# The samples' queries and scores turned in 32x32 blocks on VectorE, and another order of the pieces ahead of the feed-forward

## The chip, the cores and the metric

The kernel runs on one core of a Trainium2 chip. The metric is the device time of one execution in microseconds (us); the lower the better. A time is the median of several runs; a profile is one further execution, taken with the hardware profiler, and has a time and a span (first to last instruction) of its own.

## The reference

One layer of a decoder trunk for a prompt of 1024 tokens and 8 samples of one token each, all in float32, model width 1024:

```python
h = rmsnorm(x, g_mix); u = h @ w_in                # 512 pool, 512 value, 512 gate columns
ya = pool_mixer(...)                               # trailing means over 2/4/8/16, a map per group
yb = conv_mixer(...)                               # GLU, causal depthwise conv of 31, LayerNorm, silu
x = x + concat([ya, yb]) @ w_out
x = x + cross_attn(rmsnorm(x, g_attn), mk, mv)     # 4 heads of 256, 256 memory tokens
h = rmsnorm(x, g_ffn)
x = x + (silu(h @ w_gate) * (h @ w_up)) @ w_down   # 2816 hidden columns
y = rmsnorm(x, g_final)
```

The prompt attends to keys and values that are computed from `mem_prompt`. Each of the 8 samples attends to a cache of its own (`cache_mem_k`, `cache_mem_v`: 256 tokens, 4 heads of 256). The other outputs are the new pooling and convolution states and the prompt's keys and values.

## The kernel before

Activations lie with channels on the 128 partitions and tokens along the free axis: 1032 columns (T), 1024 of the prompt and the 8 samples last. Each matmul of two float32 operands is made of three: an operand is split into a high part (a rounded copy) and a low part (what is left), and hi x hi, hi x lo and lo x hi are added up (`PASSES`). So weights and activations are split all the time: `split` makes the high part on ScalarE or GpSimd and the low part by a subtraction on VectorE or GpSimd; `split_by_dma` makes the high part and its negative on ScalarE or GpSimd, and the low part by a DMA from GpSimd's queue that adds the original onto the negative. `BY_DMA` lists the weight blocks that take the second way. The feed-forward and its down projection use sums of blocks with fewer products (seven in place of eight).

The instructions are not issued in the order in which they stand in the code. `ORDER` is a list of pieces, each a letter and a number ("q3", "S12"); the pieces are run in that order and add tasks to a `Program` with an engine (or a choice of engines), a cost, what they read and write, and a priority by their place. `Program.order` then plans the tasks with these costs: at each step it takes the engine that can start first, and on it the earliest task, the one with the smaller place among those within a small slack; it also assigns buffers, of which each tag has a fixed number (`w` 2, `raw` 3, `scr` 3, `op` 19, `rows` 2; in PSUM `mm` 2 of three banks and `ms` 2 of one). The instructions of each engine are emitted in that order, and each engine runs its own list in order, waiting where an operand isn't there. All plain DMAs go through SP's queue, in order too. `LEAD` says how many blocks ahead of its use a weight block is prepared.

The pieces around the change:

- `q` (`q_group`): queries, 72 matmuls each; the 8 sample columns of each are copied to `qs` (L1004). `S` (`scores`, L1023), `T` (`p_transpose`, L1062) and `P` (`pv`, L1081) are the prompt's scores, the turning of the probabilities and the products with the values; the results are split into `oo` (L1085, L1086).
- `a` (`s_query`, L1090): for head h, two transposes on TensorE (L1095) turn `qs` (128 channels x 8 samples, two halves) into rows of 8 samples x 256 in PSUM; VectorE copies them out (L1099), and a DMA writes them to DRAM (`qd`).
- `b` (`s_scores`) and `d` (`s_values`), both by `s_dots`: a DMA reads the rows back, broadcast to all partitions; two DMAs bring pieces of the cache; VectorE multiplies and sums up (L1120), one sample at a time. Most heads do this in two halves of four samples with the three `scr` buffers; three of the eight (head, cache) pairs use `op` buffers and all eight samples (`ALL_SAMPLES`).
- `c` (`s_softmax`): the scores `ssc` (128 tokens x 8 samples, two halves) are turned by two transposes on TensorE (L1133); maximum (L1141), exponential (L1145) and normalising (L1150) follow on the 8 rows, which a DMA writes to DRAM (`pd`) for the values.
- `e` (`s_out`): the samples' results, in `qs` again (`os_`), are split into the last 8 columns of `oo`.
- `B` (`out_b`): second part of the mixer's output projection; makes x1, splits it for the queries, and adds its squares up. `f` (`token_factors`): the RMS factors of the tokens. `o` (`proj_o`): attention output projection, blocks 0 to 7 of 72 matmuls; for blocks 0 and 4, the first two thirds of the columns come first, and the third third, which holds the samples, after. It adds the residual (L1192) and the squares (x2sq) for the factors `Rf` (piece `r`, L510).
- `x`, `y`, `z` make the operands of the feed-forward, `h` its first weights, `i` and `j` its first products (L1323). At the end, L1665 is the last part of the down projection, with the weight blocks w_dn 16 to 19 and w_dn2 0 and 1.

Of the kernel before, what the change touches and what calls it, by code (L numbers as in the profile page):

```python
# [8 lines left out]
F32 = mybir.dt.float32  # L9
F32R = mybir.dt.float32r  # L10
AF = mybir.ActivationFunctionType
ALU = mybir.AluOpType
# [248 lines left out]
def hybrid_step_kernel(ctx: ExitStack, tc: tile.TileContext, io):  # L261
# [78 lines left out]
    pd = dram.tile([HEADS, NS, NMEM], F32, name="pd")  # L340

# [6 lines left out]
    nc.gpsimd.memset(cnt, 1.0)  # L348
# [41 lines left out]
    def split_by_dma(dst, key, src, n, r, again, again_keys, pool_too=False):  # L390
# [11 lines left out]
        add({"Pool": 0.6}, lambda e: e.dma_start(dst(1), again(), accum_op=ALU.add), [key(1)] + again_keys, [key(1)], nbytes=4 * P * n)  # L402

# [553 lines left out]
    def out_b(n):  # L957
# [11 lines left out]
        square_into(lambda: xss1[:], (xss1,), lambda: x1[j][:, i], [xk], T, n == 0, f"x1sq{n}")  # L969
# [24 lines left out]

    qop = [op_r(f"qo{n}") for n in range(KT)]
# [3 lines left out]
    def q_group(n):  # L999
# [4 lines left out]
        add({"DVE": 0.07}, lambda e: e.tensor_copy(qs[:, n], ps[:, 2, CW - NS : CW]), all3(ps), [("qs", n)])  # L1004
# [85 lines left out]
    def s_query(h):  # L1090
        ps = ms_buf(f"sq{h}")

        def emit(e):
            for dt in range(2):
                e.transpose(ps[:NS, dt * P : (dt + 1) * P], qs[:, 2 * h + dt], ident)  # L1095
# [3 lines left out]
        add({"DVE": 0.33}, lambda e: e.tensor_copy(rows[:], ps[:NS, :256]), [(ps,)], [(rows,)])  # L1099
        dma(lambda: qd[h], lambda: rows[:], 8192, r=[(rows,)], w=[("qd", h)])  # L1100

    def s_dots(h, scratch, skey, cache, out, okey):
# [5 lines left out]
        for first in range(0, NS, count):  # L1108
# [3 lines left out]
                P * count * 1024, r=[skey], w=[(bc,)])  # L1112
# [12 lines left out]
    def s_scores(h):  # L1125
        s_dots(h, qd, ("qd", h), "cache_k", lambda m: ssc[:, h, m], ("ssc", h))

    def s_softmax(h):
        ps = ms_buf(f"ss{h}")

        def emit(e):
            for m in range(2):
                e.transpose(ps[:NS, m * P : (m + 1) * P], ssc[:, h, m], ident)  # L1133

        add({"PE": 0.25}, emit, [("ssc", h, m, half) for m in range(2) for half in range(2)], [(ps,)])
        st = buf(f"sst{h}", "sst", (NS, 4))
        rs = r16[:NS, 16:17]
        prow = buf(f"prow{h}", "rows", (NS, 256))

        def top(e):  # L1140
            e.tensor_reduce(st[:, 0:1], ps[:NS, :256], axis=AX.X, op=ALU.max)  # L1141
            e.scalar_tensor_tensor(st[:, 1:2], st[:, 0:1], -1.0, rs, ALU.mult, ALU.mult)
# [703 lines left out]
```

## Time and profile before

| | |
|---|---|
| median of 3 runs | 1224.16 us (1222.42 to 1229.16) |
| the profiled execution | 1224.89 us |
| its span, first to last instruction | 1223.0 us |
| TensorE (PE) busy, matmuls | 1200.1 us, 7720 |
| VectorE (DVE), ScalarE (ACT), GpSimd (POOL) busy | 927.2, 527.8, 243.3 us |
| data moved by DMA | 181.80 MB, mean 149 GB/s |

In the profile's lines an instruction is named by its line in the code, its engine and its operands by the program's names, "out<-in". "x8" is a count. In a list of waits stand the total, the number and the longest; in a timeline, the start and the duration in us, and in brackets the idle time before it and what ended it. SPq and POOLq are the queues' own instructions, which issue DMAs. `ld` behind PE is the loading of weights into the array, which runs beside the matmuls.

### The profile page before, as it was taken

To read this page: it belongs to the slowest core of one execution; us is meant where nothing else is said; L and a number is where in the kernel's file an instruction comes from. 1 tells how busy PE (TensorE), PEld (TensorE's weight loads), DVE (VectorE), ACT (ScalarE), POOL (GpSimd) and SP (SyncE) were. 2 spreads that over 40 slices of the span, in tenths; PEclk is the share of its full clock that TensorE was granted. 3 is DMA by queue.
4 is the path that set the end of the run, shared out by engine and by line. 5 is a ranking of instruction groups with operands and counts; after the bars stand their busy time and mean duration, and the time that the engine had idled before them with its cause. 6 is when DMAs were issued, how large, how long until landed. Compare 5 with 4: busy or idle time off the path is not lost.

```text
span 1223.0 us, 19412 instructions
## 1 busy us (share of the span) xinstructions
PE 1200.1 (98%) x7720; PEld 1122.0 (92%) x7720; DVE 927.2 (76%) x1549; ACT 527.8 (43%) x722; POOL 243.3 (20%) x296
## 2 busy tenths in 40 slices
PE   8999999999999999999999999999999999999997
PEld 8999988999999979989999999999999999999786
DVE  7999999767258886679777777777867788888654
ACT  7765556455134533444222322233222365545433
POOL 3568841231111102111000000000000124332101
PEclk9999999999999999999999999999999999999998
DMA  7335678226395773421232233222313698668612
GB/s 287 86 72 114 143 210 250 105 104 194 115 294 182 240 280 103 156 104 61 104 113 79 96 113 113 105 78 96 122 70 111 217 317 239 172 183 220 155 50 90
DMA packets 60875, 181.80 MB, mean 149 GB/s; under 512 B 7857, under 2 KB 11633, under 8 KB 59505
## 3 DMA queue, kind: packets, MB, share of 16 engines
q1 hardware_dynamic: 53824, 157.92, 37.1%
q0 software_dynamic: 6960, 22.65, 10.5%
q8 instruction: 60, 0.98, 0.3%
q14 instruction: 31, 0.25, 0.1%
HBM read 146.76 MB, written 33.78 MB: 148 GB/s over the span
## 4 chain that ended last, share of the span: by engine, by line
PE 76%; DVE 4%; DMA 2%; issue 2%; ACT 1%; POOL 0%; DVEq 0%; POOLq 0%; ACTq 0%
PE pr L1323 48%; PE ps L480 7%; PE po L480 7%; PE fd L1665 5%; PE ob L480 4%; PE oa L480 3%; PE sc L1023 1%; PE pv L1081 1%; DMA w<-in_w_q 1%; DMA raw<-in_w_out_a 1%; DMA w<-in_w_dn 0%; DVE spcache_k L1120 0%; DMA spcache_k<-in_cache_k 0%; DVE oo L1086 0%; DVE pT L1067 0%
## 5 line engine op out<-in xcount | busy, mean ns | idle before, releaser
L1323 PEld LDWEIGHTS pr<-ab,wTb 128*128 128x128 f32 x1056 | 132.1, 188 | 3.6
L1323 PE MATMUL pr<-ab,wTa 128*128 128x260 f32 x1056 | 133.6, 282 | 0.0
L1323 PE MATMUL pr<-ab,wTb 128*128 128x260 f32 x1056 | 133.3, 282 | 0.0
L1323 PEld LDWEIGHTS pr<-ab,wTa 128*128 128x128 f32 x1056 | 130.7, 189 | 2.0 <-DVE su L1339 0.3
L1323 PE MATMUL pr<-ab,wG 128*128 128x512 f32 x528 | 128.8, 392 | 0.0
L1339 DVE TENSOR_TENSOR su<-pr,su 128x520 f32<-128x520 f32 (+1 forms) x112 | 77.5, 694 | 57.5 <-PE pr L1323 57.3
L480 PE MATMUL ps<-xop,w 128*128 128x344 f32 x720 | 114.1, 320 | 0.0
L480 PEld LDWEIGHTS ps<-xop,w 128*128 128x128 f32 x720 | 113.6, 188 | 0.0
L1323 PEld LDWEIGHTS pr<-ab,wG 128*128 128x128 f32 x528 | 96.3, 188 | 18.8
L1323 PEld LDWEIGHTS pr<-hb,dV 128*128 128x128 f32 x768 | 98.4, 188 | 5.8 <-ACT dV L373 0.9
L1323 PE MATMUL pr<-hb,dV 128*128 128x260 f32 x768 | 100.2, 283 | 1.0 <-DVE dV L384 0.5
L480 PE MATMUL ps<-xq,w 128*128 128x344 f32 x576 | 94.8, 321 | 0.3 <-DMA w<-in_w_q 0.3
L480 PEld LDWEIGHTS po<-oo,w 128*128 128x128 f32 x576 | 90.9, 188 | 0.6 <-DVE oo L1086 0.4
L480 PE MATMUL po<-oo,w 128*128 128x344 f32 x576 | 91.4, 320 | 0.0
L480 PEld LDWEIGHTS ps<-xq,w 128*128 128x128 f32 x576 | 90.7, 188 | 0.7 <-DMA w<-in_w_q 0.6
L684 DVE SCALAR_TENSOR_TENSOR cacc<-glu,vec,cacc 128x511 f32<-128x511 f32 (+14 forms) x116 | 76.9, 739 | 0.0
L1323 PE MATMUL pr<-hb,dW 128*128 128x512 f32 x288 | 74.2, 394 | 0.0
L1665 PE MATMUL fd<-ho,w 128*128 128x260 f32 (+1 forms) x432 | 69.8, 322 | 0.7 <-DMA w<-in_w_dn 0.6
L1665 PEld LDWEIGHTS fd<-ho,w 128*128 128x128 f32 x432 | 61.7, 188 | 8.4 <-DMA w<-in_w_dn 1.1
L373 ACT ACTIVATE w<-raw 128x1024 fp32r<-128x1024 f32 (+1 forms) x35 | 32.9, 944 | 77.1 <-issue 19.7
L1323 PE MATMUL pr<-ab,wU 128*128 128x512 f32 x264 | 64.8, 394 | 0.0
L1350 POOL MEMSET su<- 128x16 f32 x22 | 2.5, 111 | 310.0 <-PE pr L1323 244.3
(306 smaller groups left out, 2183.9 us busy)
## 6 DMA issues: line engine op xcount, KB each, us to landing
gr<-in_w_gu SPq DMA_DIRECT2D x44, 512.0 KB, 3.6
hb<-su SPq DMA_DIRECT2D x8, 1040.0 KB, 4.6
hs<-hb SPq DMA_DIRECT2D x16, 520.0 KB, 6.7
dr<-in_w_dn SPq DMA_DIRECT2D x16, 512.0 KB, 3.7
spcache_k<-in_cache_k SPq DMA_DIRECT2D x12, 512.0 KB, 5.2
hs<-hb SPq DMA_DIRECT2D x12, 512.0 KB, 4.7
raw<-in_w_in SPq DMA_DIRECT2D x10, 512.0 KB, 3.7
hb<-he SPq DMA_DIRECT2D x8, 520.0 KB, 3.2
```

What stands on the lines that cost most here:

```text
L373: e.activation(dst(0), src(), AF.Copy, scale=1.0 if gain is None else gain)
L480: e.matmul(ps[:, c, :CW], w[:, wi, cols], x[:, xi, c * CW : (c + 1) * CW], start=first and p == 0, stop=last and p == 2)
L684: e.scalar_tensor_tensor(acc[h][:, n:], src[:, : HALF - n], w, acc[h][:, n:], ALU.mult, ALU.add)
L1023: e.matmul(bank()[:, i * NMEM : (i + 1) * NMEM], qop[2 * h + dt][:, qi, tt * P : (tt + 1) * P], kk[:, ki, 2 * (h % 2) + dt], start=(dt == ...
L1081: e.matmul(ps[:, c], v[:, vi, m, col : col + P], pT[h][m][:, pi, sl], start=(m == 0 and p == 0), stop=(m == 1 and p == 2))
L1323: e.matmul(bank(c), w[:, wi, cols(j)], xs[0](j, xi)[:, c * n : (c + 1) * n], start=onto is None and j == 0 and p == 0, stop=j == nj - 1 an ...
L1339: from_sums(sums, "DVE", dve, lambda e, src, sl: e.tensor_tensor(as_banks(o(sl), src), src, as_banks(a(sl), src), op), [akey], [okey])
L1350: add({"Pool": 0.12}, lambda e: e.memset(o(), 0.0), [], keys)
L1665: e.matmul(view(i), w[:, wi, col : col + P], hops[k][:, xi, half, lo - half * HALF + i * width // count : lo - half * HALF + (i + 1) * wid ...
```

## The change

`qs` and `ssc` get another layout (head, sample, half), so that the 16 columns of a head lie together, and are set to zero at the start. `s_query` and `s_softmax` no longer use TensorE and PSUM: VectorE turns 128 x 32 columns (those of a head and its neighbour) in 32x32 blocks. In the result a partition holds 32 channels (or tokens) of one sample and half. For the queries, four DMAs of 2 KB (one for each group of 32 partitions) write the rows in order to `qd`; for the scores, one DMA writes the whole 128 x 32 tile to a new DRAM tensor `sd`, and a second one reads the 8 x 256 rows back in order; the softmax then works on these rows in SBUF.

The squares in `out_b` and `proj_o` become pieces of their own (`t`, `u`), and the last third of blocks 0 and 4 of `proj_o` too (`E`), so that `ORDER` can place them. `ORDER`, `BY_DMA` and `LEAD` get other entries.

```diff
 ORDER = (
-    "m5 A3 n0 g1 v1 g2 v2 m3 m7 m4 C0 g3 v3 C1 m0 s1 s0 A2 m1 D0 A0 m2 m6 A1 K0 K1 V1 W3 D1 W0 K2 s3 s2 W1 W2 C2 M0 M3 V0 "
-    "C3 D2 D3 M1 L0 M2 K3 O0 O1 O3 O2 B0 B1 B2 B3 q0 q1 Z0 a0 b0 f0 q2 c0 q3 a1 b1 c1 S4 S0 S6 S5 S2 q4 q5 a2 Y0 S7 S1 S3 "
-    "S8 T0 d0 T3 T4 S9 T1 S10 T2 d1 q6 T8 q7 S11 T11 T5 P1 S12 T10 a3 S15 S13 T9 S14 T12 b2 T7 T6 T13 b3 T14 T15 c3 c2 d2 "
-    "P4 e1 e0 P5 P2 P3 P7 d3 P0 e3 P6 e2 o0 o4 o1 y0 o5 x0 x1 x4 o2 h0 x5 z0 h1 y1 o6 o3 x2 o7 z1 h2 y2 x6 x3 y3 x7 z2 r0 "
-    "h3 i1 i0 j0 z3 j1"
+    "m1 n0 m5 A3 m7 g1 m3 v1 g2 v2 g3 v3 A1 C0 C1 A2 s1 m2 s0 D0 m6 A0 m4 m0 K1 D1 V1 K0 W3 W0 K2 s3 W1 C2 s2 M0 W2 M3 V0 "
+    "C3 D2 D3 M1 L0 K3 M2 O0 O1 O2 O3 B3 B0 t0 B1 t1 t2 B2 t3 t4 t5 q0 t6 t7 q1 Z0 f0 q3 a0 b0 q2 a1 b1 S0 S4 c0 c1 S6 Y0 "
+    "S5 S7 q5 S3 q4 a2 S2 S1 T0 S8 d0 T2 T3 T4 S9 T1 d1 b2 T5 S10 q6 T8 q7 S11 P1 T11 S12 S13 S14 T10 S15 T9 T12 T7 T6 a3 "
+    "b3 c3 T14 c2 d2 e0 e2 e1 P0 d3 T15 T13 P4 P5 P2 P6 P7 P3 o0 o4 e3 E0 E4 x4 y0 o5 x0 u0 u4 o1 u1 z0 u5 x5 y1 h0 h1 o2 "
+    "o6 u2 u6 y2 o3 x2 u3 o7 h2 h3 x1 x3 x6 z1 i1 u7 r0 y3 x7 z2 i0 j0 z3 j1"
 )
-BY_DMA = {"w_in": (3, 4, 6, 7, 9, 10, 11), "w_k": (2, 3, 5, 6), "w_o": (4, 5, 6), "w_out_a": (1,), "w_out_b": (3,), "w_q": (4, 5, 6), "w_v": (0, 7), "w_dn": (17, 18, 19), "w_dn2": (1,)}
+BY_DMA = {"w_in": (3, 4, 5, 6, 7, 9, 10, 11), "w_k": (2, 3, 5, 6), "w_o": (0, 2, 4, 6), "w_out_a": (1, 3), "w_out_b": (0,), "w_q": (2, 3, 4, 5, 6), "w_v": (0, 1, 6, 7), "w_dn": (18,), "w_dn2": (1,)}
-LEAD = {"w_k": 2, "w_v": 3, "w_out_a": 15, "w_q": 15, "w_in": 1, "w_out_b": 12, "w_o": 8}
+LEAD = {"w_k": 2, "w_v": 3, "w_out_a": 14, "w_q": 18, "w_in": 2, "w_out_b": 10, "w_o": 5}
...
-    qs = const.tile([P, KT, NS], F32, name="qs")
-    os_ = qs
-    ssc = const.tile([P, HEADS, 2, NS], F32, name="ssc")
+    qs = const.tile([P, HEADS, NS, 2], F32, name="qs")
+    ssc = const.tile([P, HEADS, NS, 2], F32, name="ssc")
...
+    sd = dram.tile([HEADS, P, 32], F32, name="sd")
...
+    nc.gpsimd.memset(qs, 0.0)
+    nc.gpsimd.memset(ssc, 0.0)
...
+    def turned(name, src, h, r):
+        t = buf(f"{name}{h}", "rows", (P, 32))
+        add({"DVE": 0.12}, lambda e: e.transpose(t[:], src[:, min(h, 2) : min(h, 2) + 2].rearrange("p h b i -> p (h b i)")), r, [(t,)])
+        return t
...
     def s_query(h):
-        ps = ms_buf(f"sq{h}")
-        def emit(e):
-            for dt in range(2):
-                e.transpose(ps[:NS, dt * P : (dt + 1) * P], qs[:, 2 * h + dt], ident)
-        add({"PE": 0.25}, emit, [("qs", 2 * h), ("qs", 2 * h + 1)], [(ps,)])
-        rows = buf(f"qrow{h}", "rows", (NS, 256))
-        add({"DVE": 0.33}, lambda e: e.tensor_copy(rows[:], ps[:NS, :256]), [(ps,)], [(rows,)])
-        dma(lambda: qd[h], lambda: rows[:], 8192, r=[(rows,)], w=[("qd", h)])
+        t = turned("qt", qs, h, [("qs", 2 * h), ("qs", 2 * h + 1)])
+        for g in range(4):
+            dma(lambda g=g: qd[h].rearrange("b (i g d) -> (b i) g d", i=2, g=4)[:, g], lambda g=g: t[32 * g + 16 * (h == 3) : 32 * g + 16 * (h == 3) + 16], 2048,
+                r=[(t,)], w=[("qd", h, g)])
...
     def s_softmax(h):
-        ps = ms_buf(f"ss{h}")
-        def emit(e):
-            for m in range(2):
-                e.transpose(ps[:NS, m * P : (m + 1) * P], ssc[:, h, m], ident)
-        add({"PE": 0.25}, emit, [("ssc", h, m, half) for m in range(2) for half in range(2)], [(ps,)])
+        t = turned("st", ssc, h, [("ssc", h, m, half) for m in range(2) for half in range(2)])
+        dma(lambda: sd[h], lambda: t[:], 128 * P, r=[(t,)], w=[("sd", h)])
...
+        dma(lambda: prow[:].rearrange("b (m g d) -> b m g d", m=2, g=4),
+            lambda: sd[h].rearrange("(g z b m) d -> z b m g d", g=4, z=2, b=NS)[int(h == 3)], 8192, r=[("sd", h)], w=[(prow,)])
...
-            e.tensor_reduce(st[:, 0:1], ps[:NS, :256], axis=AX.X, op=ALU.max)
+            e.tensor_reduce(st[:, 0:1], prow[:], axis=AX.X, op=ALU.max)
```

More of the change, by code (lines that the diff above doesn't have):

```diff
@@ L402, in split_by_dma, with took @@
         add({"Pool": 0.6}, lambda e: e.dma_start(dst(1), again(), accum_op=ALU.add), [key(1)] + again_keys, [key(1)], nbytes=4 * P * n)
+    def took(name):
+        state[name] = state.get(name, -1) + 1
+        return state[name]
     def square_into(total, tkey, src, r, n, first, name, at=None):
@@ L968, in out_b, with x1_square @@
         dma(lambda: x1d[n], lambda: x1[j][:, i], 4 * P * T, r=[xk], w=[("x1d", n)])
-        square_into(lambda: xss1[:], (xss1,), lambda: x1[j][:, i], [xk], T, n == 0, f"x1sq{n}")
+    def x1_square(n):
+        j, i = n // 2, n % 2
+        square_into(lambda: xss1[:], (xss1,), lambda: x1[j][:, i], [(x1[j], i)], T, not took("t"), f"x1sq{n}")
     def token_factors():
@@ L1155, in s_values @@
     def s_values(h):
[L1156 removed]
+        s_dots(h, pd, [("pd", h)], "cache_v", lambda dt: qs[:, h, :, dt], ("os", h))
     def s_out(h):
@@ L1186, in proj_o, with spans_of, o_out, x2_square @@
         ps = mm_buf(f"po{n}")
-        for spans in ((0, 1), (2,)) if n in (0, 4) else ((0, 1, 2),):
+        def spans_of(spans):
+            parts = [0] * (0 in spans) + [1] + ["s"] * (2 in spans)
             for k in range(KT):
-                parts = ([0] if 0 in spans else []) + ([1, "s"] if 2 in spans else []) + ([0, 1] if spans == (0, 1) else [])
                 okeys = [(oop[k], p, part) for part in parts for p in range(2)]
                 step3(ps, w, wkeys, block_cols(k), oop[k], k, k == 0, k == KT - 1, spans, okeys)
+        if n in (0, 4):
+            spans_of((0, 1))
+            late_o[n] = lambda: (spans_of((2,)), o_out(n, ps))
+        else:
+            spans_of((0, 1, 2))
+            o_out(n, ps)
+    late_o = {}
+    def o_out(n, ps):
+        j, i = n % 4, n // 4
+        xk = [(xa[j], i, h) for h in range(2)]
         add({"DVE": dve(T)}, lambda e: e.tensor_tensor(ch3(xa[j][:, i]), ps[:, :, :CW], ch3(xa[j][:, i]), ALU.add), all3(ps) + xk, xk)
         dma(lambda: x2d[n], lambda: xa[j][:, i], 4 * P * T, r=xk, w=[("x2d", n)])
-        square_into(lambda: xss2[:], (xss2,), lambda: xa[j][:, i], xk, T, n == 0, f"x2sq{n}")
+    def x2_square(n):
+        j, i = n % 4, n // 4
+        square_into(lambda: xss2[:], (xss2,), lambda: xa[j][:, i], [(xa[j], i, h) for h in range(2)], T, not took("u"), f"x2sq{n}")
     def quarter(j, i, h):
```

19 lines of the change are left out of this document (9 added, 10 removed).

## The prediction

> **What bounds the kernel now.** I read the page first (busy times and the slices), then what TensorE waited for, then the stretches in which it waited.
>
> ```profile
> span 1223.0 us, 19412 instructions
> PE 1200.1 (98%) x7720; PEld 1122.0 (92%) x7720; DVE 927.2 (76%) x1549; ACT 527.8 (43%) x722; POOL 243.3 (20%) x296
> PEclk9999999999999999999999999999999999999998
> ```
>
> TensorE is busy for 1200.1 of 1223.0 us at a full granted clock, so the time is its work plus 22.9 us of idle. The list of its waits says where 14.3 us of these are:
>
> ```profile
> PE psg L480 <- ACT w L373: 5.2, 1, 5.2
> PE pv L1081 <- DVE oo L1086: 2.1, 2, 1.2
> PE Rf_ps L510 <- DVE xss L411: 1.8, 1, 1.8
> PE kps L850 <- DMA w<-in_w_k: 1.1, 2, 0.7
> PE pmap L870 <- ACT yf L874: 0.9, 1, 0.9
> PE fd L1665 <- DMA w<-in_w_dn: 0.6, 1, 0.6
> PE fin_ps L1699 <- ACT fsq L1680: 0.6, 1, 0.6
> PE pr L1323 <- DVE dV L384: 0.5, 1, 0.5
> PE pr L1323 <- ACT dV L373: 0.5, 1, 0.5
> PE ps L480 <- DMA w<-in_w_q: 0.3, 1, 0.3
> PE sc L1023 <- ACT probs L1040: 0.3, 1, 0.3
> PE Rx_ps L510 <- DVE Rx_m L512: 0.2, 1, 0.2
> PE oa L480 <- DVE opa L384: 0.2, 1, 0.2
> ```
>
> The columns are total, times and longest wait in us. The start (5.2), Rx (0.2), the end (0.6) and what is left for the tail after the last matmul (22.9 - 14.3 = 8.6) no edit touches. Open to another order, other loads or another split of weights are pv 2.1, Rf 1.8, kps 1.1, pmap 0.9, fd 0.6, dV 1.0, w_q 0.3, sc 0.3, oa 0.2: together 8.3 us. Two stretches show it by engine (columns: length, then busy time of PE, weight load, DVE, ACT, POOL):
>
> ```profile
> 413.00:450.00 37.00, 34.48 (x192) 28.10 (x191) 30.91 (x91) 22.13 (x50) 2.11 (x7) 1.00 0.73 251
> 549.00:1131.00 582.00, 582.00 (x3883) 536.21 (x3882) 458.56 (x653) 208.96 (x268) 57.17 (x92) 1.00 0.44 137
> ```
>
> From 413 to 450 us TensorE lacks 2.5 us beside a VectorE that is busy for 30.9 of 37.0. From 549 to 1131 us, the feed-forward, it lacks nothing and the change touches nothing.
>
> **The change, part by part.**
>
> *TensorE's turns for the samples go.* Each head had a pair of transposes for the query and a pair for the scores.
>
> ```profile
> 348.87 0.22 PE sq L1095 x2
> 367.56 0.22 PE ss L1133 x2
> ```
>
> Eight pairs of 0.22 us in the chain of work: -1.8 us, certain as far as TensorE sets the end, which it does for 98% of the span. Two PSUM buffers ("ms") that scores and probabilities share are also no longer taken eight times; I count that in the waits below.
>
> *VectorE.* Four copies of 0.40 us (8x256 out of PSUM) go, eight block transposes of 128x32 come. No row shows one.
>
> ```profile
> 421.13 0.40 DVE L1099 COPY qrow<-sq 8x256 f32<-8x256 f32 x1
> 411.83 0.17 DVE L1004 COPY qs<-ps 128x8 f32<-128x8 f32 x1 [0.18 <-PE ps L480]
> ```
>
> Bounds: the 128x8 copy at 0.17 and the 256-wide copy at 0.40 us. I take 0.2, by its width nearer to the first: 8 x 0.2 - 4 x 0.40 = 0.0 us, between -0.2 and +1.6; VectorE has 6.1 us of slack in the stretch above, so 0 on the end. [...]
>
> *The DMAs.* The blocks come out with rows of 32 numbers, so the query takes four DMAs instead of one, and the scores go out to DRAM and back before the softmax: two hops that were not there. 16 + 4 + 4 DMAs replace 4 (the write of the probabilities stays): 20 more issues on SP.
>
> ```profile
> 421.57 0.29 SPq L359 DMA_DIRECT2D qd<-qrow  x1
> 424.40 9.66 SPq L359 DMA_DIRECT2D sbcache_k<-qd  x2
> 446.68 0.29 SPq L359 DMA_DIRECT2D pd<-prow  x1
> out_pool_p<-a SPq DMA_DIRECT2D x4, 8.0 KB, 3.5
> ```
>
> A hop is what SP waits between the write and the read behind it: 424.40 - 421.57 = 2.8 us for the query. A small write in short pieces (8 KB of pooling state) took 3.5 us to land. I take 2.8 a hop, 5.6 for two, with 3.5 (7.0) as the upper end. [...]
>
> *Who waits for the longer hop.* While the scores travel, the first reduction of the softmax waits on VectorE, and behind it in that queue stand the evacuations of scores and of P times V that TensorE needs back. SP waits too: the read stands until the write has landed, and weights and caches queue behind it. On the path to the end is head 3, the last:
>
> ```profile
> 440.44 2.85 DVE spcache_k L1120 x16
> 444.42 0.40 DVE L1141 TENSOR_REDUCE sst<-ss 8x1 f32<-8x256 f32 x1
> 459.44 0.43 DVE L1120 SCALAR_TENSOR_TENSOR spcache_v<-spcache_v,sbcache_v 128x256 f32<-128x256 f32 x1 [0.81 <-DMA sbcache_v<-pd]
> 465.42 0.20 POOL L384 TENSOR_TENSOR oo<-qs,oo 128x8 fp32r<-128x8 f32 x1
> 450.39 81.41 PE po L480 x513
> 470.62 1.23 DVE L1192 TENSOR_TENSOR xa<-po,xa 128x1032 f32<-128x1032 f32 x1 [5.57 <-PE po L480]
> ```
>
> Head 3's dots with K end at 443.3, its softmax starts at 444.4, its values are split by 465.6. The output projection starts at 450.4 and runs at 81.41 / 513 = 0.159 us a matmul. Blocks 0 and 4 run first without the third span, 96 matmuls, to 465.6; the 36 matmuls of the third span that need no head 3 reach to 471.3. So head 3 may be late by 471.3 - 465.6 = 5.7 us before TensorE stops. The change makes it later by 5.6 us of hops, less the 1.1 us from 443.3 to 444.4 in which it waited for TensorE's transpose, plus three issues at 0.29: +5.4. And TensorE arrives earlier by what is saved ahead of 450 us (4.2, below). Unmoved, the stop would be 5.4 + 4.2 - 5.7 = 3.9 us. Against it: head 3's query stood from 411.83 to 421.13 until TensorE's and VectorE's turn came, and the new order puts b2 right behind d1, so K tiles of head 2 no longer stand in head 3's way; up to 9.3 us could come back, and the stop be 0. I take 2.0, about the middle. Apart from that, taking the third span out as pieces E0 and E4 costs nothing: same matmuls, and the two PSUM buffers of blocks 0 and 4 were held as long before.
>
> *The order and the weights.* Moved pieces carry their DMAs with them; the work of each queue stays the same but for BY_DMA.
>
> ```profile
> w<-in_w_q POOLq DMA_DIRECT2D x3, 512.0 KB, 8.5
> 338.05 10.04 DMA w<-in_w_q
> 1146.96 1.06 ACT L395 ACTIVATE w<-w 128x1024 fp32r<-128x1024 f32 x1
> 322.97 1.23 DVE L384 TENSOR_TENSOR w<-raw,w 128x1024 fp32r<-128x1024 f32 x1 [0.97 <-ACT w L373]
> ```
>
> Seven more blocks ahead of the feed-forward (w_in 1, w_v 2, w_q 2, w_o 1, w_out_a 1) get their low part by an accumulating DMA, which lands after 8.5 us where VectorE's subtraction took 1.23: each frees 1.2 us of VectorE and is ready some 7 us later. There are two w buffers, so one block is prepared while one is worked on: a block of w_q is 72 matmuls of 0.159 us, 11.4 us, and two scalings on ScalarE and 8.5 us just fit. The one wait of this kind (w_q, 0.3 us) had a DMA of 10.04 us before it. I take 0; the upper end is 2 blocks of w_q by 10.04 + 2.1 - 11.4 = 0.7, +1.4 us. Of the final w_dn, 17 and 19 go back to a subtraction. What I expect of the 8.3 us: fd's 0.6 goes, since it ended with this landing, issued at 1146.28:
>
> ```profile
> 1146.28 0.87 POOL L402 DMA_DIRECT2D w<-in_w_dn  x1 [7.41 <-ACT w L395]
> 1152.12 28.44 PE fd L1665 x136
> ```
>
> The subtraction in its place is 1.23 us of VectorE (row above), beside other work. dV's 1.0 us stays: nothing moves in it. For the rest nothing in the profile tells which wait the new order makes; each can go wholly or come back elsewhere, so I take half: the samples' stretch (pv, sc, w_q: 2.7) -1.3; keys, values and mixer (kps, pmap, oa: 2.2) -1.1; the handoff to the feed-forward (Rf 1.8) -0.9, where squares u0 to u7 now have places of their own. What is ahead of 450 us is then 1.8 + 1.3 + 1.1 = 4.2.
>
> *At nothing:*
>
> ```profile
> 1.33 0.15 POOL L348 MEMSET cnt<- 128x64 f32 x1
> 3.77 0.55 POOL L375 TENSOR_SCALAR xop<-xraw,vec 128x344 fp32r<-128x344 f32 x1 [1.31 <-DMA xraw<-in_xT]
> ```
>
> Two more memsets of this size on GpSimd, which stands idle for 1.31 us at the start until x lands, the strides of qs and ssc, the reduction and exponential from SBUF instead of PSUM (same 8x256), LEAD. Without that cover the memsets would cost 0.3 us.
>
> **The sum.** -1.8 - 0.6 - 1.3 - 1.1 - 0.9 + 2.0 = -3.7 us on a span of 1223.0. The profiled execution took 1224.9 in all, 0.7 above the median of 1224.16; so 1224.16 - 3.7 = 1220.5 us.
>
> **Rivals.**
> - *All waits close.* Head 3 comes early enough (a3 no longer needs TensorE) and the order closes all 8.3 but dV's 1.0: -1.8 - 7.3 = -9.1, 1215. For: pv's 2.1 us stand directly beside these transposes. Against: VectorE has as much to do in that stretch as before.
> - *The gain is eaten by head 3.* The stop is the full 3.9 us, or with 3.5 us a hop 5.3: -5.7 + 3.9 to 5.3 = -1.8 to -0.4, 1222.4 to 1223.8. Where the order closes nothing ahead, TensorE comes only 1.8 earlier: -2.4 + 1.5 to 2.9 = -0.9 to +0.5, 1223.3 to 1224.7. For: nothing in the profile says that head 3 begins earlier. Against: the 9.3 us that its query stood. [...]
> - *Slower: VectorE stands in line for the scores.* In 413 to 450 us the softmaxes of heads 2 and 3 lie between evacuations of pv. A row that lands 5.0 us late (two hops less some lead) stops the queue, and TensorE's cover is already used up: it waits 2.1 us for pv today. Two heads: +10.0 - 1.8 - 0.6 = +7.6, 1232. It decides from where the reduction stands less than two hops behind its transpose in VectorE's queue. For: a hop on the chip is long, and a DMA of K was waited for in just that place. Against: V of head 2 does not press, so its softmax can stand later.
> - *It doesn't do what it says* cannot be: the transposes on TensorE are gone from the text.
>
> **Chances.** Forecast (1217 to 1222) 0.42; all waits close (1213 to 1217) 0.16; eaten (1222 to 1228) 0.18; slower (1228 to 1240) 0.24. The range 1213 to 1234 leaves out the worse part of the last and a rest below. 0.5% is 6.1 us, about what a measurement of this kernel can tell from no change. Faster (below 1218.0): 0.16 and 0.10 of the forecast, 0.26. Slower (above 1230.3): 0.22 of the last. Same: 0.52.
>
> **What would show it.** Matmuls 7704 instead of 7720 and no rows of ss and sq under PE; pv's wait below 2.1 and fd's gone; a wait of po on the samples' split (oo from qs) between 450 and 475 us is the stop I put at 2.0; a wait of VectorE's L1141 on the DMA of prow is the slower rival, and pv behind it its price. Wrong I would be if waits for weights grew instead, w_k or w_in by accumulating DMA among them, or if the feed-forward no longer ran without gaps.

## The result, and the profile after

The kernel after took 1230.39 us (median of 22 runs, 1223.59 to 1239.53) beside 1224.04 us for the kernel before on the same chips (22 runs, 1221.80 to 1229.79): 1.0048 times as long, 95% interval 1.0028 to 1.0068, so slower by about 5.9 us (the medians differ by 6.4), and with twice the spread. The profiled execution took 1230.24 us, close to the median, so its trace is compared with that of before; how far one trace stands for this kernel is taken up in experiments 3 and 5.

The busy time and the granted clock on the page of the kernel after:

```profile
PE 1198.6 (98%) x7704; PEld 1122.1 (91%) x7704; DVE 924.5 (75%) x1550; ACT 531.5 (43%) x726; POOL 247.6 (20%) x302
PEclk9999999999999989999999999999999999999999
```

TensorE has the 16 matmuls less and is 1.5 us less busy. But the span is 1228.5, so its idle time grew from 22.9 to 29.9 us, and one slice in the middle has an 8 in the clock. The list of what TensorE waited for (total, times, longest):

```profile
PE pt L1078 <- DVE pT L1083: 5.9, 2, 4.7
...
PE kps L857 <- DVE w L386: 2.7, 1, 2.7
PE Rf_ps L517 <- DVE xss L418: 1.6, 1, 1.6
PE pv L1097 <- DVE oo L1102: 1.6, 1, 1.6
...
PE po L487 <- POOL w L386: 0.8, 1, 0.8
PE sc L1039 <- ACT probs L1056: 0.8, 1, 0.8
...
PE pt L1078 <- DVE probs L1064: 0.6, 1, 0.6
PE sc L1039 <- DVE pT L1083: 0.5, 1, 0.5
```

The rows left out are the start (psg, 5.2 as before and 1.0 for a second operand) and the end (fin_ps, 0.6 as before). fd and dV are gone, pv fell from 2.1 to 1.6, Rf from 1.8 to 1.6. New is 4.7 us of pt on VectorE's pT, and kps grew from 1.1 to 2.7. Where the time goes is read from the chain of work, in which the same stages stand in both traces; first before, then after (start, duration):

```profile
299.07 22.72 PE ps L480 x144
548.61 583.25 PE pr L1323 x3887
```

```profile
297.85 22.73 PE ps L487 x144
555.80 585.36 PE pr L1347 x3894
```

The queries start 1.2 us earlier, the feed-forward 7.2 us later, and the end is 5.5 us later. So the stretch from the queries to the feed-forward loses 8.4 us, and everything else gains 2.9, 1.7 of it in the tail. In the profiled execution the waits of that stretch grew from 4.5 us (pv 2.1, Rf 1.8, sc 0.3, w_q 0.3) to 11.8 (the rows above without kps), +7.3; the transposes are 1.8 less; and the half clock below costs 2.0. That makes 7.5 of the 8.4.

The 4.7 us on VectorE's and on TensorE's timeline of after:

```profile
431.36 0.42 DVE L1130 SCALAR_TENSOR_TENSOR spcache_k<-spcache_k,sbcache_k 128x256 f32<-128x256 f32 x1 [5.31 <-DMA sbcache_k<-qd]
...
433.61 1.28 DVE L1083 TENSOR_TENSOR pT<-pt,pT 128x512 fp32r<-128x512 f32 x2
```

```profile
426.61 3.06 PE L1097 MATMUL pv<-pT,vv 128*128 128x512 f32 x12
434.35 1.97 PE L1078 MATMUL pt<-ident,probs 128*128 128x128 f32 x8 [4.67 <-DVE pT L1083]
435.96 4.16 PE L1097 MATMUL pv<-pT,vv 128*128 128x512 f32 x12
439.96 1.04 PE L1078 MATMUL pt<-ident,probs 128*128 128x128 f32 x8
```

VectorE stands idle for 5.31 us at head 3's first product with its cached keys, because the query's broadcast (`sbcache_k<-qd`) is not there. Behind it in VectorE's queue stands pT, the split of the prompt's turned probabilities, for which TensorE waits. After the stop the same 8 transposes take 1.97 instead of 1.04 us and the same 12 matmuls 4.16 instead of 3.06: 2.0 us more. The stretch's row (the number after POOL's is the granted clock) says why:

```profile
430.00:439.00 9.00, 4.66 (x16) 4.09 (x17) 7.33 (x26) 3.26 (x9) 2.43 (x7) 0.62 0.50 163
```

A mean of 0.62 over 9 us is a clock at half for 0.38 x 9 / 0.5 = 6.8 us; in slices of 1 us it stands at 0.50 from 432 to 438 and at 1.00 again from 439. The length of a stop alone does not say how long the half clock behind it is: kps' 2.7 us here bring none (1.00 from 150 to 190), its 2.8 us in e8 3.4 us of it (a mean of 0.57 from 175 to 179), and in e12 a stop of 1.9 us, with 0.7 us more behind it, brought 6.8 us (0.62 from 364 to 373). What else decides it was not shown.

Why is the query late? SP's queue in after, first head 0, then head 3:

```profile
321.75 0.35 SPq L361 DMA_DIRECT2D raw<-in_w_q  x1
322.14 1.34 SPq L361 DMA_DIRECT2D qd<-qt  x3
325.93 0.34 SPq L361 DMA_DIRECT2D sbcache_k<-qd  x1
```

```profile
415.70 0.33 SPq L361 DMA_DIRECT2D qd<-qt  x1
416.08 0.41 SPq L361 DMA_DIRECT2D raw<-in_w_o  x1
416.54 1.36 SPq L361 DMA_DIRECT2D qd<-qt  x3
418.00 0.49 SPq L361 DMA_DIRECT2D spcache_v<-in_cache_v  x1
425.45 0.34 SPq L361 DMA_DIRECT2D sbcache_k<-qd  x1
```

The read waits for the writes to land; head 3's wait is in the chain of work itself, and ends at 425.32, just ahead of the read at 425.45 (start, duration):

```profile
417.48 7.84 DMA qd<-qt
```

From the end of the last write's issue to the read it is 2.4 us for head 0 (322.14 + 1.34 = 323.48 to 325.93) and 7.6 us for head 3 (417.90 to 425.45). In both, a weight load of 512 KB stands between the first and the other three writes: one write had become four, and the plan put a load between them; head 3 has a cache load ahead of its read too.

### The profile page after: what moved, and what is told of

The parts are those of the page before. It is cut to its first block, busy times and chain, and to the rows that moved or that the text cites. A ratio compares the mean times of both kernels' runs of the same rounds, so it can differ in the third digit from the quotient of the medians.

```text
span 1228.5 us, 19426 instructions
## 1 busy us (share of the span) xinstructions
PE 1198.6 (98%) x7704; PEld 1122.1 (91%) x7704; DVE 924.5 (75%) x1550; ACT 531.5 (43%) x726; POOL 247.6 (20%) x302
## 4 chain that ended last, share of the span: by engine, by line
PE 85%; DVE 7%; DMA 6%; issue 1%; ACT 1%; SPq 0%; POOL 0%; DVEq 0%; POOLq 0%; ACTq 0%
PE pr L1347 48%; PE ps L487 13%; PE fd L1689 5%; PE po L487 5%; PE oa L487 4%; PE ob L487 4%; DVE spcache_v L1130 1%; DVE spcache_k L1130 1%; DMA sbcache_k<-qd 1%; DMA spcache_k<-in_cache_k 1%; DMA qd<-qt 1%; PE kps L857 1%; PE vps L934 1%; PE psv L487 1%; DMA spcache_v<-in_cache_v 1%
## 5 line engine op out<-in xcount | busy, mean ns | idle before, releaser
L1363 DVE TENSOR_TENSOR x<-pr,x 128x512 f32<-128x512 f32 (+1 forms) x76 | 52.3, 691 | 13.6 <-PE pr L1347 12.6
```

The lines of the kernel that those rows point to most:

```text
L1363: from_sums(sums, "DVE", dve, lambda e, src, sl: e.tensor_tensor(as_banks(o(sl), src), src, as_banks(a(sl), src), op), [akey], [okey])
```

## The experiments

**1. Either part alone (e1 to e4).** e1 is the change without the new order, e2 the new order without the turns on VectorE; e3 and e4 are the kernel after with only the queries, or only the scores, turned on TensorE as before.

```diff
# e1: the kernel after, but
-ORDER = ("m1 n0 m5 A3 m7 g1 ...")       # with t, u, E; BY_DMA, LEAD
+ORDER = ("m5 A3 n0 g1 v1 g2 ...")       # all three as before
# e2: the kernel before, but with after's ORDER, BY_DMA, LEAD and the pieces t, u, E
# e3: the kernel after, s_query as before
-        t = turned("qt", qs, h, ...)
+                e.transpose(ps[:NS, dt * P : (dt + 1) * P], qs[:, h, :, dt], ident)
# e4: the kernel after, s_softmax as before
-        t = turned("st", ssc, h, ...)
+                e.transpose(ps[:NS, m * P : (m + 1) * P], ssc[:, h, :, m], ident)
```

e1: 

> The kernel before with the turns on VectorE and the regrouping DMAs alone; order, weights by DMA, lead, squares and block pieces as before. Theory A (the query's small writes queue on SP behind weight and cache loads, VectorE stands waiting for head 3's rows, TensorE stops behind it): if the order puts a load among or just ahead of the four writes of head 3, about 1228 to 1230 us with a VectorE wait on the broadcast of the queries of several us; else about 1224. Theory B (the two softmax hops hold VectorE): 1228 to 1230 with the wait on the softmax rows. Theory C (the new order and weights alone made it slower): 1222 to 1223, the transposes' 1.8 us gained.

e2: 

> The kernel before with the new order, weights by DMA, lead and the pieces for squares and blocks 0 and 4 alone; the turns stay on TensorE. Theory A and B: no long hop, so about 1222 to 1225 us and no stop of several us between 420 and 440. Theory C: 1229 to 1231, the same stop as in the changed kernel.

e3: 

> The changed kernel with the queries turned on TensorE as before (one write of 8 KB a head); the scores' turn and both softmax hops stay. Theory A: the stop of 4.7 us at head 3 and the slow clock behind it go, about 1223 to 1225 us. Theory B: stays at 1229 to 1231.

e4: 

> The changed kernel with the scores turned on TensorE as before, without the two softmax hops; the queries' turn on VectorE and the four small writes a head stay. Theory A: the stop stays, 1228 to 1231 us. Theory B: 1223 to 1225.

Measured, as ratios to the kernel before: e1 1235.13 us, 1.0096 [1.0078, 1.0113]; e2 1244.96 us, 1.0181 [1.0161, 1.0202]; e3 1244.78 us, 1.0178 [1.0155, 1.0200]; e4 1234.78 us, 1.0089 [1.0060, 1.0118]. Each half is slower than the whole, e4 only just (its interval touches that of after). Each stops at places of its own: e1 at po for the samples' results (row below), e2 and e3 at the key weights (kps, 6.9 and 6.7 us), e4 at sc for the split of the queries (4.2 us).

```profile
PE po L482 <- DVE oo L386: 2.3, 1, 2.3
```

The chain of work ahead of e2's stop at the key weights goes through one copy of VectorE, which in the same run takes 0.17 us elsewhere:

```profile
151.39 7.36 DVE L811 COPY side<-a 128x8 f32<-128x8 f32 x1
```

It ends with GpSimd's window step at 158.7; in e3 it takes 7.20 us, in after 2.3. How the two engines hold each other is the subject of part 5. So these two runs price this hold as well as the part that they leave out.

The planner works out the whole schedule from the tasks, so taking out one part moves everything, key weights 100 us ahead of the samples included. My theories in the form that they had here fell, as each wanted one of the four near 1224; what the runs do show is that `ORDER` fits only the set of tasks for which it was made. From here on I changed the plan only after it was made, one thing at a time. e1 and e3 also have the stop that the prediction put into its sum: po waits for the split of the samples' results, 2.3 us in e1, 2.3 and 1.7 us in e3.

**2. Which hop (e5, e6).** In e5 the broadcasts of all queries read an input tensor instead of `qd`, so they wait for no write and the samples' scores are of other numbers; in e6 the softmax's rows come from an input instead of `sd`, so its rows wait for no write and are other numbers. All instructions and their order stay.

```diff
# e5: in s_dots, where cache is cache_k
-    lambda first=first: scratch[h : h + 1, first : first + count] ...
+    lambda first=first: io["w_q"][h][0:1, ...] (or io["cache_k"][h][0:1]) ...
# e6: in s_softmax
-    lambda: sd[h].rearrange("(g z b m) d -> z b m g d", ...)[int(h == 3)]
+    lambda: io["w_q"][h].rearrange("(g z b m) d -> z b m g d", ...)[int(h == 3)][:, :, :, :32]
```

e5: 

> The changed kernel, every instruction in its place, but the broadcast that feeds the samples' dots with K reads a constant part of an input instead of the queries just written, so that nothing waits for the four small writes to land (the samples' scores are then other numbers). It prices the whole query hop, in all heads. Theory A' (the query hop, queued behind loads, holds SP, then VectorE, then TensorE): 1222 to 1225 us, TensorE's stop of 4.7 us gone. Theory B (the softmax hop): 1229 to 1231. Theory C' (the new order's own waits, in the keys' stretch and around the scores): 1228 to 1230.

e6: 

> The changed kernel, every instruction in its place, but the softmax rows are read from a constant part of an input instead of the scores just written, so that the second hop waits for nothing (the samples' probabilities are then other numbers). It prices the softmax hop. Theory B: 1223 to 1226 us. Theory A' and C': 1229 to 1231, since the rows land in front of a VectorE that TensorE does not wait for.

e5: 1231.65 us, 1.0064 [1.0041, 1.0086]. e6: 1230.35 us, 1.0057 [1.0038, 1.0077]. So the landing of one hop's write is not the cost by itself. But this doesn't clear the hops, since they stand side by side: the scores' write of head 0 and the four query writes of head 1 go out within 4 us, among the same weight and cache loads, and on SP's queue the read of the scores' rows stands ahead of the broadcast of head 1's queries. In e5, where the broadcast waits for no write, the chain of work goes through the scores' write:

```profile
350.46 8.61 DMA sd<-st
```

The broadcast leaves behind it at 359.98, and TensorE stops 2.1 us at sc, with 6.8 us of half clock. In e6 it is the other way round: the softmax's rows wait for no write, but the broadcast still leaves 5.6 us behind head 1's last query write, and VectorE still waits 4.0 us for the rows (3.7 in after), whose read stands behind a cache load. At head 3 of e5 the broadcast is still behind 512 KB of weights and a cache load, and TensorE stopped 1.6 us for pT. So the suspect is the order of the loads, for writes and reads alike.

**3. The order of the loads (e7, e8).** After the planning, e7 moves the weight load behind the fourth small write (heads 0, 1 and 3), e8 moves it and the value-cache loads that stand between the writes and the read behind the read. Head 2 stays as it is in both.

```diff
     plan = pg.order()
+    for h in (0, 1, 3):
+        first = ...  # place of the first write of qd[h];  read = place of the first sbcache_k<-qd[h]
+        stop = ...   # e7: the last write of qd[h];  e8: read
+        for x in [x for x in plan[first:stop] if x is a load of raw (e8: or of spcache, but not of the head's own K) on SP]:
+            plan.insert(stop, plan.pop(plan.index(x)))
```

e7: 

> The changed kernel with the same plan, except that the 512 KB weight load that stands on SP between the first and the other three small writes of heads 0, 1 and 3 is issued behind the fourth. Theory A': the writes land some 2.5 us after their issue instead of up to 8, the read behind them is issued earlier, but its 512 KB then stand behind the loads: 1226 to 1229 us. Theory B and C': 1229 to 1231.

e8: 

> As the one before, and these weight loads and the loads of the V cache that follow (1 MB for head 3) are issued behind the read of the queries instead of ahead of it. Theory A': 1222 to 1226 us, VectorE's wait of 5.3 us for the queries of head 3 is below 2. Theory B and C': 1229 to 1231, or slower where the later loads are missed.

e8: 1225.76 us (1221.40 to 1235.74, 12 runs), 1.0021 [1.0002, 1.0041], 4.6 us under after. Its queue at head 3, and the stretch after:

```profile
416.78 1.71 SPq L361 DMA_DIRECT2D qd<-qt  x4
420.79 0.34 SPq L361 DMA_DIRECT2D sbcache_k<-qd  x1
```

```profile
430.00:439.00 9.00, 9.00 (x49) 7.55 (x48) 7.63 (x24) 5.53 (x13) 2.17 (x7) 1.00 0.87 311
```

The read follows 2.3 us (418.49 to 420.79) behind the last write instead of 7.6, and TensorE works through the nine microseconds in which it was busy for 4.66. This gap varies between executions. Taken in the same way from the SP rows of all traces of this plan, six with the loads where the plan has them (after, e6, e9, e11, e12, e13) and five with e8's edit (e8, e10, e14, e15, e16), and from the one trace of before, the last write to the read in us:

| head | before, one write | loads as planned | loads behind the read |
|---|---|---|---|
| 0 | 2.6 | 2.4 to 2.8 | 1.1 to 1.1 |
| 1 | 3.1 | 3.4 to 7.7 | 3.0 to 3.9 |
| 2 (not moved) | 11.9 | 7.9 to 9.8 | 8.7 to 9.8 |
| 3 | 2.5 | 3.6 to 7.6 | 2.3 to 4.7 |

Head 2 is the control: nothing was moved there, and its range hardly changed. So the 7.6 us of after's trace are the upper end of a range, and in the mean the edit takes 1.4, 2.6 and 1.4 us off the gaps of heads 0, 1 and 3.

Which head TensorE pays for differs between executions. The stop of 4.7 us at pT is in after's trace alone; the longest in the other five is 1.0 to 1.7 us, and with e8's edit it is 0.9 to 1.5. In e11, e12 and e13 it is head 1 that is late, with gaps of 7.4 to 7.7 us, and TensorE stops 1.9 to 2.6 us at sc, with 3.4 to 6.8 us of half clock behind it. In e12's chain of work the last query write takes 7.95 us to land (first row), the broadcast 4.68, and VectorE's products with K stand ahead of what ScalarE and then TensorE (second row) wait for:

```profile
346.97 7.95 DMA qd<-qt
```

```profile
363.85 2.06 PE L1039 MATMUL sc<-kT,qo 128*128 128x256 f32 x12 [1.87 <-ACT probs L1056]
```

All six traces with the loads as planned have this wait of sc for ScalarE's probs, 0.8 to 2.8 us in total; none of the five with the loads behind the read has it. Cut at the same two stages as above, the traces come out so (us):

| | to the queries | queries to feed-forward | feed-forward to the end |
|---|---|---|---|
| before | 299.1 | 249.5 | 674.4 |
| loads as planned (6) | 295.6 to 303.7 | 252.2 to 258.0, mean 255.1 | 672.7 to 673.3 |
| loads behind the read (5) | 296.0 to 303.2 | 250.6 to 251.3, mean 250.9 | 672.8 to 673.3 |

In the middle stretch the two groups don't overlap. Of the 5.5 us that it is longer than before, the order of the loads makes 4.2, and with it nearly all of the scatter of this stretch (5.7 us against 0.7); why the last 1.3 us stay, with 1.8 us less of transposes, is open. The first column scatters with either order; its stops are the subject of parts 4 and 5.

e7, the weaker edit, did not help: 1237.69 us (1230.72 to 1241.33, 6 runs), 1.0106 [1.0080, 1.0133], though its gaps are like e8's at heads 0 and 3 (1.1, 2.3). In e7 the broadcast itself still stands behind the loads, as in e5. Its one trace is of its fastest execution, with 255.4 us in the middle stretch, as with the loads as planned. Why its median is above that of after stays open.

**4. The stop at the key weights (e9, e10).** kps waits for VectorE's subtraction that makes a weight block's low part. e9 is after with that subtraction ahead of the window sums in VectorE's queue, e10 is e8 with it.

```diff
+    lo = place of w_k 4's subtraction;  first = place of the first window mean (both on VectorE)
+    plan.insert(first, plan.pop(lo))
```

e9: 

> The kernel after with the same plan but for one instruction: VectorE's low-part subtraction of one key-weight block (w_k 4, 3.67 us beside GpSimd's window work at 170.4, where others of its shape take 1.22) stands ahead of the window sums' mean at 165.0 instead of behind them. Nothing is left out. Theory G (the 2.7 us stop of kps at 173.5, and the half-clock stretch that follows it in some runs, are a second part of the loss): the stop is gone, the window sums and vv's subtraction come 1.2 us later with slack of over 100 us for vv, and the time falls by 2.7 to 4.5 us against the kernel after, to 1226 to 1228; the runs scatter less. Rival H (the stop is only moved: what is behind the subtraction, kf or the window products, ends late instead): a stop of 1 to 3 us at pmap or at the next kps, and 1229 to 1232. Rival I (the half clock is not tied to this stop): the stop is gone, the time falls by 2.7 at most, and the runs scatter over 1222 to 1240 as those of the kernel after.

e10: 

> The kernel after with both moves: the raw weight and V-cache loads behind the read of the queries on SP's queue (as in e8), and the key-weight subtraction ahead of the window means (as in e9). Nothing is left out. If the two losses are separate and add (theory F+G): 1225.8 less 2.7 to 4.5, so 1221 to 1223, a little under the kernel before (1224.0), with no stop of TensorE over 1.7 us and no half clock before the last 10 us. If what remains in e8 is the run's general scatter of clock (rival I): 1223 to 1226, the same as e8 within its interval.

e9: 1232.32 us (1223.83 to 1238.06, 12 runs), 1.0058 [1.0035, 1.0082]; e10: 1225.56 us (1221.99 to 1234.70, 12 runs), 1.0020 [0.9997, 1.0044]. No gain over after and e8: the runs of e9 are as rival I had them, and theory G's gain did not come. Yet e9's profiled execution took only 1223.83 us, 8.5 below its median, and in it the stop at kps was gone: one trace of such a kernel says little about its median.

**5. The same kernels again (e11, e12).** No edit: e9's kernel and after's, for a second trace each.

e11: 

> The same kernel as e9 once more, for the trace of another execution: its profiled execution took some 1224, its median 1232. Theory J (stops of 1 to 2 us in the samples' stretch, with the granted clock then half for 3.4 or 6.8 us, come and go between executions, since how long the small transfers take behind the loads on SP's queue varies): an execution of 1230 or more shows one or more stretches of half clock between 340 and 450 behind a wait of VectorE for a transfer, and nothing new elsewhere. Rival K (something before the samples, for instance the start or the key weights, varies): its half clock or its stops lie before 300.

e12: 

> The kernel after once more, for the trace of another execution. Theory J: the stop of 4.67 us at 434 is smaller or larger with the moment at which the queries of head 3 land, other stops of the samples' stretch change too, and the stop of kps at 173.5 stays near 2.7 us, since it waits for an instruction of VectorE and for no transfer; the half-clock stretches lie behind the larger stops. Rival K: the samples' stops are the same within 0.3 us and the difference between the executions lies before 300.

e11 took 1234.41 us, e12 1226.75, one execution each (the kernel before took 1229.36 beside them). Neither theory has it all: e11 has one half clock of 3.4 us at 373, behind the samples, and another at 185, behind the keys; in e12 the stop at 434 shrank to 1.0 us, as theory J wanted, but the stop of kps, which I had called steady, shrank from 2.7 to 0.2 us. VectorE (first) and GpSimd (second) in the trace of after:

```profile
169.74 3.67 DVE L386 TENSOR_TENSOR w<-raw,w 128x1024 fp32r<-128x1024 f32 x1
```

```profile
168.96 0.90 POOL L824 COPY win<-a 128x1 f32<-128x1 f32 x1
169.83 1.27 POOL L825 TENSOR_TENSOR win<-a 128x511 f32<-128x511 f32 x1
171.07 1.25 POOL L826 TENSOR_TENSOR win<-a 128x512 f32<-128x512 f32 x1
```

And the same in e12:

```profile
170.06 1.22 DVE L386 TENSOR_TENSOR w<-raw,w 128x1024 fp32r<-128x1024 f32 x1
```

```profile
169.37 0.82 POOL L824 COPY win<-a 128x1 f32<-128x1 f32 x1
170.16 2.27 POOL L825 TENSOR_TENSOR win<-a 128x511 f32<-128x511 f32 x1
```

In either trace one of the two engines is held while the other works. In after it is VectorE's subtraction, 3.67 us, which ends 1.1 us behind GpSimd's last addition, and TensorE waits for it; in e12 it is GpSimd's addition, 2.27 us, and nobody waits. Seen by their starts the two cases are alike, the subtraction beginning in GpSimd's copy, 0.1 us ahead of its next addition: a toss. What the two hold each other by was not shown; what the traces have is the length: 3.67 us for a subtraction that takes 1.22 otherwise, 2.27 for an addition of GpSimd that takes 1.27. The copy in e2 (part 1), with one input only, was held too, 7.36 us beside 0.17. The convolution's sums on VectorE, whose accumulator is in PSUM, are not stretched beside GpSimd: all 116 of them in the kernel before take 723 to 749 ns, 0.66 us from one to the next, and six of these run beside GpSimd's first window steps (VectorE, then GpSimd):

```profile
156.30 3.96 DVE L684 SCALAR_TENSOR_TENSOR cacc<-glu,vec,cacc 128x502 f32<-128x502 f32 x6
```

```profile
157.98 1.59 POOL L818 TENSOR_TENSOR win<-a 128x511 f32<-128x511 f32 x1
```

e11 shows the toss lost one instruction later, and who waits then:

```profile
170.43 3.78 DVE L836 SCALAR_TENSOR_TENSOR win<-win,a 128x1032 f32<-128x1032 f32 x1
```

```profile
PE pmap L879 <- DVE kf L863: 4.7, 2, 4.0
```

**6. GpSimd's window steps on VectorE (e13 to e16).** e13 gives the step at 169 to VectorE, in after; e14 the same in e8; e15 gives all three window steps of this stretch, in e8; e16 is e15 with e9's move.

```diff
+    n = place of the window step ("win", 1, 1)       # e15, e16: also (3, 1) and (3, 2)
+    plan[n] = (plan[n][0], "DVE")                    # planned on GpSimd
```

e13: 

> The kernel after with the same plan, but the first step of one window sum (a copy and two additions, 2.9 to 3.6 us on GpSimd at 169) runs on VectorE at its place in the plan, behind the product kf. Nothing is left out. Theory L (a lottery: where this step ran on GpSimd, an instruction of VectorE beside it took 3.67 or 3.78 us instead of 1.22 in four executions and 1.22 in two, and when it was the long one TensorE stopped for 2.7 to 4 us at kps or pmap): no instruction of VectorE over 2 us between 160 and 200, no stop over 1 us before 300, and the median falls by 1.5 to 3 us against the kernel after, to 1227 to 1229. Rival H (VectorE has no room there: 1.5 us more on it delays the next product): a stop of 1 to 2 us stays at pmap or kps, and 1229 to 1232.

e14: 

> The same with the loads behind the read of the queries as in e8. Nothing is left out. Theory F+L (both losses are separate): 1225.8 less 1.5 to 3, so 1223 to 1224, about the kernel before, and a spread between executions no wider than the kernel before's 8 us. If what is left of the loss is a third thing, the chances of the many short stops of the samples' stretch, then 1225 to 1226, as e8 and e10, with a spread of 12 us or more.

e15: 

> e14 with two more window steps taken from GpSimd to VectorE (all three that GpSimd does there), the loads behind the read of the queries as in e8; same plan else, nothing left out. In e14's trace the lottery had only moved one step earlier: an addition of VectorE (0.68 us elsewhere) took 6.28 us beside GpSimd's window steps at 159 to 165, and TensorE stopped 3.5 us at kps. Theory L: no instruction of VectorE over 2 us between 150 and 200; the low part of w_k comes some 2.8 us later than in e13 for VectorE's own work, so a steady stop of 0.5 to 2 us at kps; median 1222 to 1224, spread under 8 us. Rival (VectorE is the bound of this stretch): a steady stop of 2 to 4 us, 1225 to 1228.

e16: 

> e15 with the low part of that key weight ahead of the window means, as in e9. Nothing is left out. Theory L: kps no longer waits for it; the products kf come up to 3 us later and pmap may stop for 1 us; median 1221 to 1223, spread under 8 us: a version a little faster than the kernel before (1224). Rival (VectorE is the bound of this stretch): pmap stops 2 to 4 us, 1224 to 1227.

| loads as planned | us (runs) | ratio to before | loads behind the read | us (runs) | ratio to before |
|---|---|---|---|---|---|
| after | 1230.39 (22) | 1.0048 [1.0028, 1.0068] | e8 | 1225.76 (12) | 1.0021 [1.0002, 1.0041] |
| e9 | 1232.32 (12) | 1.0058 [1.0035, 1.0082] | e10 | 1225.56 (12) | 1.0020 [0.9997, 1.0044] |
| e13 | 1230.25 (12) | 1.0038 [1.0013, 1.0062] | e14 | 1223.90 (12) | 0.9997 [0.9977, 1.0018] |
| | | | e15 | 1225.61 (12) | 1.0003 [0.9986, 1.0020] |
| | | | e16 | 1225.47 (12) | 1.0009 [0.9992, 1.0026] |

Each row changes only the loads from left to right, and each falls by 4.6 to 6.8 us. The two intervals of a pair overlap each time; that all three pairs fall, and that the traces of part 3 part where the loads act, makes the case. From top to bottom little happens: e13 alone did not come to its 1227 to 1229, and e14 is the only one under 1225. The spread of e14 is 9.6 us (1220.24 to 1229.83), that of e15 7.2, of e16 9.4, where e8's is 14.3; but e13 keeps 13.6. In the traces the toss is plain: executions without a stop over 1 us at the keys (e9, e10, e12, e13) reach the queries at 295.6 to 296.1 us, after and e14 with one at 297.9 and 299.6, e11 with two at 303.7. What it is worth in the median, 0.1 us (e13 against after) to 1.9 (e14 against e8), is not shown beside these intervals. e14's trace shows the toss at the step before: VectorE's addition, then the first of GpSimd's, and what TensorE waits for:

```profile
159.99 6.28 DVE L826 TENSOR_TENSOR win<-a 128x511 f32<-128x511 f32 x1
```

```profile
159.69 1.56 POOL L826 TENSOR_TENSOR win<-a 128x511 f32<-128x511 f32 x1
...
163.57 2.14 POOL L823 TENSOR_TENSOR win<-win 128x1022 f32<-128x1022 f32 x1
```

```profile
PE kps L860 <- DVE w L386: 3.5, 1, 3.5
```

6.28 us for what takes 0.68: it ends at 166.27, GpSimd's last window step at 165.71. With all steps on VectorE there is no such instruction any more, but TensorE still waits for VectorE there, 2.5 us at kps in e15 and 4.7 us at pmap in e16, and the times are those of the rival that has VectorE as the bound of the stretch.

No version was found that beats the kernel before.

## Why the prediction was wrong

Forecast was 1220.5 us, a little faster; it came out 1230.4, a little slower. The sum put the stretch from the queries to the feed-forward at -2.0 us (-1.8 - 1.3 - 0.9 + 2.0); it came out at +5.5 in the mean of six traces, against the one of before. By its steps:

- **TensorE's turns, -1.8: right in kind.** 7704 matmuls, 1.5 us less busy, although 2.0 us of half clock stand in that busy time.
- **VectorE's block transposes at 0.2 us: right.** All four of a kind, shortest, median and longest in ns, with the first and last start:

```profile
L1008 DVE STREAM_TRANSPOSE qt<-qs x4: 204/212/215, 320.8 to 415.5; 128x32 f32<-128x32 f32 x4
```

- **A hop at 2.8 to 3.5 us: too small.** It was read where a single write has only a cache load behind it. Here the scores' writes took 4.6, 4.3, 1.4 and 1.4 us to their reads (the second is below), and head 3's query 9.8 us from the first write to the read (rows above). The size of the pieces is not the reason: with no load among them, the four writes of head 0 take 2.8 us from the first to the read (e8), the one write of before 3.0.

```profile
364.98 0.32 SPq L361 DMA_DIRECT2D sd<-st  x1
...
369.23 0.71 SPq L361 DMA_DIRECT2D prow<-sd  x1
```

- **"SP waits too: the read stands until the write has landed, and weights and caches queue behind it": the step that failed.** It has the queue only one way round. Weights and caches also stand ahead, and between four writes a load fits that a single write has no room for. e8, which changes this alone, took off 4.6 us, the other two pairs of the last table 6.8 and 6.4, and in the traces it is 4.2 us of the stretch from the queries to the feed-forward. That is shown for the loads ahead of the read as a group; how it divides between the delay of the writes and that of the broadcast is not, since e5 and e7 each removed a part and gained nothing.
- **Head 3 late for the output projection, +2.0: wrong place.** po waits 0.8 us, for a weight. The late hop was paid earlier: in after the product with K stands in VectorE's queue ahead of pT, so TensorE stops at 434, not at 471; in e11 to e13 it is the product of head 1, and TensorE stops at sc at 364 to 372. I had traced only who needs the samples' result, not what is queued behind the instruction that waits for the query. The slower rival did so, and its sign is there: VectorE's reduction waits for the rows in after (below: total, times, longest). That its price is near the loss (7.6 us; the stretch lost 8.4 in that trace) is partly luck: it had two stops of pv behind the scores' rows, but pv's wait fell, and the stops came at pT and sc, with the queries' rows last in after and e12 and the scores' write last only where the queries wait for nothing (e5).

```profile
DVE sst L1148 <- DMA prow<-sd: 4.7, 2, 3.7
```

- **fd's 0.6 gone: right; dV's 1.0 stays: wrong.** It went as well, and the tail gained 1.7.
- **Half of the other waits close, -3.3: wrong as a rule.** Of the named ones pv gave 0.5 and Rf 0.2 back, pmap's 0.9 and oa's 0.2 went, but kps grew by 1.6 in this trace and the samples' stretch got new ones. With the loads moved, e8's trace still has pv 1.6, Rf 1.7, a new 0.8 of po and 1.4 of pt. A half taken for want of a reason also left out the half clock behind a stop, 2.0 us here.
- **BY_DMA at 0: right in the place named.** No wait for a w_q by DMA is in after's list.

## What to carry to other kernels

Before you make one small transfer into several, read what the planner puts between them on the queue: here the hop took 1.1 us with no load about it and up to 7.7 with two, for the same bytes. Charge a late operand to everything behind the waiting instruction in its engine's queue. And where an order is fitted to a set of tasks, neither half of a change can be judged alone: change one thing in the finished plan instead, and take a second trace before a stop is explained.

## What the runs showed of the hardware

- VectorE and GpSimd held each other up: 3.67, 3.78 and 6.28 us for instructions of VectorE that take 1.22, 1.23 and 0.68 us otherwise, and 2.27 us (e12) for one of GpSimd that takes 1.27. In e14 one instruction of VectorE lasted 6.28 us through five of GpSimd on end, and in e2 a 128x8 copy that takes 0.17 us elsewhere took 7.36.
- Which of the two is held differs between executions of one kernel (after and e12), and with it a stop of 2.7 us. Over 22 runs each the kernel before spread over 8 us and after over 16; beside e9, the kernel before spread over 11.5 in 23 runs.
- Four writes of 2 KB let the read behind them go 1.1 us after the last one's issue at head 0 with no load among them, and 2.4 to 2.8 us with 512 KB among them; at head 3 the same plan took anything from 3.6 to 7.6 us.
- A stop of 4.7 us cost 2.0 us more through a half clock of 6.8 us; in e12 a stop of 1.9 us and one of 0.7 behind it came with as long a half clock, in after one of 2.7 us with none.
